# Moving the weight pool of a decoder trunk by 192 bytes, so that its tiles start at the same byte modulo 512 as the transposed input

## The chip, the cores and the metric

The kernel runs on one core of one Trainium2 chip. The metric is device microseconds of the whole program, the median of several runs.

## What is computed

The reference is a decoder trunk of four post-norm layers on 512 tokens of width 1024, in float32. Layers come in the pattern mixer, MLP, mixer, MLP; after each one stands a layer norm of 4^(1/4)·x plus the layer's output.

```python
# mixer 0: stick-breaking attention (8 heads) beside a complex diagonal SSM (32 groups), one output projection
x = layer_norm(ALPHA * x + mixer_sb_ssm(x), ...)
x = layer_norm(ALPHA * x + square(relu(x @ w1[0])) @ w2[0], ...)
# mixer 1: an indexer scores all keys, each query keeps its 128 best, 16 heads attend to those (ALiBi)
x = layer_norm(ALPHA * x + mixer_dsa(x), ...)
x = layer_norm(ALPHA * x + square(relu(x @ w1[1])) @ w2[1], ...)
```

## The kernel before

Every large product is made in three matmuls. A float32 operand is split into a high part in the fp32r type and a low remainder; `mm3` (L129 to L133) then accumulates high·high (L131), high·low (L132 or L133) and low·high. TensorE reads a moving operand of 512 columns, 2048 bytes in each partition, and a stationary operand of 128 columns, 512 bytes in each partition, from SBUF.

Who is moving and who is stationary differs by place:

- Projections to feature-major form (`proj_fm`, the SSM input, the gate): the transposed input `xhi`, `xlo` moves, and the weights `whi`, `wlo` are stationary (L131 to L133). With 512 columns this is the SSM input (`psu`), the queries and keys of both mixers, and groups 1 to 7 of each MLP's first matrix. Group 0 of each MLP and the indexer's projections (`psi`) run in halves of 256 columns.
- Blocks in token-major form: weights move and the activations are stationary. These are the values of mixer 0 (L750 to L752), the output projections (L716 to L718, stationary `xhi`, `xlo`) and the MLP's second matrix (L255 to L257, stationary `hhi`, `hlo`).

Weights pass through three kinds of tile: `raw` (DMA from HBM), `whi` (cast on ScalarE, L104) and `wlo` (remainder, L105). They come from one of two places: the pool "w", which lives through the whole kernel, or a pool that the MLP opens for itself. In the MLP the first matrix's group 0 and nearly all of the second matrix use the MLP's own pool; groups 1 to 7 of the first matrix, and half 0 of the second matrix's last group (48 matmuls in each MLP), use pool "w".

Pools on the left side are stacked in the order in which they are opened: "const", "w", "ln", "x", then each mixer's own. So the size of "const" sets the byte at which everything after it begins, while `xhi`, `xlo`, the MLP's tiles and the SSM's stand on the right side and are not moved by it. Before the change, the start addresses modulo 512, as the built program has them, are:

| tiles | start modulo 512 |
|---|---|
| `xhi`, `xlo` | 480 |
| `raw`, `whi`, `wlo` of pool "w" | 288 |
| the MLP's own `raw`, `whi`, `wlo`, and `hhi`, `hlo` | 480 |
| `ident` | 192 |
| attention tiles `qst`, `kst`, `wt`, `aw` of mixer 0 | 96 to 192 |

Matmul slices start at whole multiples of 512 bytes inside these tiles (the indexer's 64-column key weights apart), so a slice has the residue of its tile.

The order of the work is set by a scheduler that simulates the program as it is built; dependences between tiles, including the reuse of a buffer, shape that order. Around the change it matters in `top_keys` (L981 to L994). For the query blocks it is given, it repeats 16 times: VectorE's MAX (L988) takes the 8 largest scores of a row from `acc` into `top`, and MATCH_REPLACE (L989) overwrites those 8 in `acc`. Block 1 is treated first and alone; blocks 2 and 3 (384 and 512 columns wide) are treated together. `top` has four buffers. When both are done, L993 and L994 make the distance tile `dist` of each block, and `sparse_attention` begins: TensorE makes logits (L1011), VectorE adds `dist` and finds the row minimum (L1018).

Of the kernel before, what the change touches and what calls it, by code (L numbers as in the profile page):

```python
# [8 lines left out]
F32 = mybir.dt.float32  # L9
F32R = mybir.dt.float32r  # L10
AF = mybir.ActivationFunctionType
# [4 lines left out]
P = 128  # L16
# [19 lines left out]
class Trunk:  # L36
    def __init__(self, ctx, tc, a, out):
        self.ctx, self.tc, self.nc, self.a, self.out = ctx, tc, tc.nc, a, out
        self.n = self.n_mlp = self.na = 0
        self.marks = {}  # L40
        self.kept = False
        nc = self.nc
        cp = self.cp = ctx.enter_context(tc.tile_pool(name="const", bufs=1))
        top = ctx.enter_context(tc.tile_pool(name="top", bufs=1, side="right"))
        cp.tile([P, 16], F32, name="pad")
        self.wp = ctx.enter_context(tc.tile_pool(name="w", bufs=1))
        self.psa = ctx.enter_context(tc.tile_pool(name="psa", bufs=1, space=PSUM))
        self.psb = self.psc = None
        self.lnp = ctx.enter_context(tc.tile_pool(name="ln", bufs=1))
        self.xhi = top.tile([P, KT, S], F32R, name="xhi")  # L50
        self.xlo = top.tile([P, KT, S], F32R, name="xlo")
        self.ident = cp.tile([P, P], F32, name="ident")
        self.ident_r = cp.tile([P, P], F32R, name="ident_r")
        self.mhalf = cp.tile([P, 1], F32, name="mhalf")
        self.zero = cp.tile([P, 1], F32, name="zero")
        nc.gpsimd.memset(self.mhalf, -0.5)
        nc.gpsimd.memset(self.zero, 0.0)
        nc.gpsimd.memset(self.ident, 0.0)
        nc.gpsimd.affine_select(out=self.ident, in_=self.ident, pattern=[[-1, P]], compare_op=ALU.not_equal,
                                fill=1.0, base=0, channel_multiplier=1)  # L60
        nc.vector.tensor_copy(self.ident_r, self.ident)
        warm = cp.tile([P, 1], F32, name="warm")
        nc.scalar.activation(warm, self.zero, AF.Exp)

    def open_psb(self):
        self.psc = None
# [914 lines left out]
    def top_keys(self, qbs, ip, accs, drm, dist):  # L981

        vec = self.nc.vector
        for step in range(TOPK // 8):
            for qb in qbs:
                acc = accs[qb]
                top = ip.tile([P, 8], F32, tag="top", bufs=4, name=self.nm("top"))
                vec.max(top, acc)  # L988
                vec.match_replace(acc, top, acc, MARK)  # L989
        for qb in qbs:  # L990
            nk = (qb + 1) * P
            acc = accs[qb]
            vec.tensor_scalar(acc, acc, -3.2e38, BIG, ALU.is_gt, ALU.mult)  # L993
            vec.tensor_tensor(dist[:, qb, :nk], acc, drm[:, S - nk:], ALU.max)  # L994
# [82 lines left out]
```

## Time and profile before

| | |
|---|---|
| median of 3 runs | 1201.22 us (1200.93 to 1202.5) |
| the profiled execution's own time | 1200.24 us |
| its span, first to last instruction | 1198.4 us |
| mean granted TensorE clock | 0.989 |
| TensorE matmul busy | 1157.1 us (97%) |
| VectorE busy | 718.7 us (60%) |
| ScalarE, GpSimd busy | 442.7 us (37%), 192.7 us (16%) |
| chain that ended last, by engine | PE 82%, DVE 11%, DMA 3% |

How to read it: matmuls overlap in the pipe, and the end of one is modelled, so the duration of a matmul row (about 390 ns) is no measure of pace. The distance from the start of one matmul to the start of the next is; it is read from the timeline, whose first column is the start. VectorE rows have real durations. The two MLPs take roughly 250 to 610 us and 835 to 1190 us of the span, mixer 0 the time before, mixer 1 the time between.

### The profile page before, as it was taken

Reading aid. Unit: us, or ns where it says so; the run is one execution under the profiler, and the core shown is the slowest. Engines: PE = TensorE matmul, PEld = TensorE weight load, DVE = VectorE, ACT = ScalarE, POOL = GpSimd, SP = SyncE. Lnnn points to the kernel's source line nnn. Section 1 sums busy time; section 2 is a strip of 40 time slices with the busy share of each in tenths; the row PEclk is TensorE's granted clock in tenths of the full one; section 3 lists DMA queues with packets and bytes.
Section 4 is the critical chain, followed back from the end, with each engine's and each line's share of the span. In section 5 each row is a group of like instructions: output and inputs, shape, how many; then the busy total and the mean of one; then the engine's idle time right before and its main releaser. Section 6 shows DMA issues by size and latency. Waiting matters only on the chain.

```text
span 1198.4 us, 15778 instructions
## 1 busy us (share of the span) xinstructions
PE 1157.1 (97%) x6004; PEld 953.6 (80%) x6004; DVE 718.7 (60%) x1183; ACT 442.7 (37%) x734; POOL 192.7 (16%) x209
## 2 busy tenths in 40 slices
PE   7999998999999999999999989998999999999997
PEld 6878776798888888888898867777988888888886
DVE  7997598675443444444567997559544444444436
ACT  5534486323322332332135457552332332322320
POOL 1044130450000000000021654337000000000001
PEclk9999999999999999999999989999999999999999
DMA  7536772633332332322145850025332332332101
GB/s 239 140 85 142 195 227 54 184 115 106 106 104 72 106 106 71 106 88 54 40 124 142 220 159 1 1 78 175 118 106 71 106 106 73 103 110 83 54 1 71
DMA packets 147307, 127.00 MB, mean 106 GB/s; under 512 B 24352, under 2 KB 115296, under 8 KB 147232
## 3 DMA queue, kind: packets, MB, share of 16 engines
q1 hardware_dynamic: 145552, 123.59, 35.9%
q10 hardware_dynamic: 1680, 2.41, 0.6%
q8 instruction: 47, 0.77, 0.3%
q14 instruction: 28, 0.23, 0.1%
HBM read 105.80 MB, written 5.37 MB: 93 GB/s over the span
## 4 chain that ended last, share of the span: by engine, by line
PE 82%; DVE 11%; DMA 3%; issue 2%; ACT 1%; SPq 1%; POOLq 0%; DVEq 0%; POOL 0%; ACTq 0%
PE psa L133 11%; PE psa L132 11%; PE psa L131 11%; PE psb L257 10%; PE psb L256 10%; PE psb L255 10%; PE pso L824 3%; PE pst L817 2%; PE psl L1011 2%; DVE acc L989 2%; PE psb L716 2%; PE psb L718 2%; PE psb L717 2%; DVE top L988 2%; DVE acc L956 1%
## 5 line engine op out<-in xcount | busy, mean ns | idle before, releaser
L104 ACT CAST whi<-raw 128x1024 fp32r<-128x1024 f32 (+1 forms) x177 | 184.0, 1046 | 490.9 <-PE psb L257 251.2
L105 DVE TENSOR_TENSOR wlo<-raw,whi 128x1024 fp32r<-128x1024 f32 (+1 forms) x142 | 179.7, 1267 | 201.2 <-ACT whi L104 200.8
L132 PE MATMUL psa<-xlo,whi 128*128 128x512 f32 (+1 forms) x720 | 271.6, 378 | 2.4 <-DVE xlo L203 2.4
L133 PE MATMUL psa<-xhi,wlo 128*128 128x512 f32 (+1 forms) x720 | 272.3, 379 | 0.0
L131 PE MATMUL psa<-xhi,whi 128*128 128x512 f32 (+1 forms) x720 | 270.6, 378 | 0.2 <-ACT xhi L202 0.2
L255 PE MATMUL psb<-whi,hhi 128*128 128x512 f32 (+1 forms) x520 | 201.0, 387 | 0.0
L256 PE MATMUL psb<-wlo,hhi 128*128 128x512 f32 (+1 forms) x520 | 200.8, 386 | 0.0
L257 PE MATMUL psb<-whi,hlo 128*128 128x512 f32 (+1 forms) x520 | 193.4, 387 | 0.0
L132 PEld LDWEIGHTS psa<-xlo,whi 128*128 128x128 f32 x720 | 137.1, 190 | 29.4 <-DVE xlo L203 2.6
L262 DVE TENSOR_TENSOR x<-x,psb 128x512 f32<-128x512 f32 (+1 forms) x105 | 69.2, 679 | 150.4 <-PE psb L257 150.2
L133 PEld LDWEIGHTS psa<-xhi,wlo 128*128 128x128 f32 x720 | 137.2, 191 | 27.0
L131 PEld LDWEIGHTS psa<-xhi,whi 128*128 128x128 f32 x720 | 136.6, 191 | 26.8 <-ACT xhi L202 0.5
L105 POOL TENSOR_TENSOR wlo<-raw,whi 128x1024 fp32r<-128x1024 f32 x35 | 93.5, 2684 | 145.8 <-ACT whi L104 136.4
L255 PEld LDWEIGHTS psb<-whi,hhi 128*128 128x128 f32 x520 | 97.7, 188 | 20.1
L256 PEld LDWEIGHTS psb<-wlo,hhi 128*128 128x128 f32 x520 | 97.7, 188 | 20.1
L257 PEld LDWEIGHTS psb<-whi,hlo 128*128 128x128 f32 x520 | 97.6, 188 | 20.1
L184 POOL TENSOR_TENSOR rs<-rs,mhalf 128x1 f32<-128x1 f32 x16 | 21.1, 1317 | 415.4 <-DVE rs L183 415.4
L716 PE MATMUL psb<-whi,xhi 128*128 128x512 f32 x128 | 50.7, 401 | 2.0 <-DVE x L721 2.0
L717 PE MATMUL psb<-wlo,xhi 128*128 128x512 f32 x128 | 50.5, 394 | 0.8 <-DVE wlo L105 0.8
L718 PE MATMUL psb<-whi,xlo 128*128 128x512 f32 x128 | 50.6, 396 | 0.0
L225 DVE TENSOR_TENSOR hlo<-h,hhi 128x512 fp32r<-128x512 f32 x64 | 44.2, 692 | 6.7 <-DVE h L223 0.5
L223 DVE TENSOR_TENSOR h<-r 128x512 f32<-128x512 f32 x64 | 43.8, 684 | 6.9 <-ACT r L222 6.9
(240 smaller groups left out, 1473.6 us busy)
## 6 DMA issues: line engine op xcount, KB each, us to landing
raw<-in_w_dram SPq DMA_DIRECT2D x128, 512.0 KB, 4.1
raw<-in_w_in_dram SPq DMA_DIRECT2D x29, 512.0 KB, 4.4
raw<-in_w_out_dram SPq DMA_DIRECT2D x16, 512.0 KB, 4.7
qst<-hl SPq DMA_DIRECT2D x48, 128.0 KB, 2.9
kst<-hl SPq DMA_DIRECT2D x24, 256.0 KB, 4.6
gb<-in_ln_g_dram SPq DMA_DIRECT2D x4, 512.0 KB, 3.6
gb<-in_ln_b_dram SPq DMA_DIRECT2D x4, 512.0 KB, 5.2
x<-in_x_dram SPq DMA_DIRECT2D x4, 512.0 KB, 6.0
```

The source lines that it names most:

```text
L104: nc.scalar.copy(hi[:, c], raw[:, c])
L105: (eng or nc.vector).tensor_tensor(lo[:, c], raw[:, c], hi[:, c].bitcast(F32), ALU.subtract)
L131: mm(ps, lhi, rhi, start=start, stop=False)
L132: mm(ps, lhi, rlo, start=False, stop=False)
L133: mm(ps, llo, rhi, start=False, stop=stop)
L255: nc.tensor.matmul(ps, lh, whi, start=f + i == 0, stop=False)
L256: nc.tensor.matmul(ps, lh, wlo, start=False, stop=False)
L257: nc.tensor.matmul(ps, ll, whi, start=False, stop=f == 3 and i == len(parts) - 1)
L262: nc.vector.tensor_tensor(xs, xs, ps, ALU.add)
L716: nc.tensor.matmul(ps, chi[:, k, tok], whi, start=i == 0, stop=False)
L717: nc.tensor.matmul(ps, chi[:, k, tok], wlo, start=False, stop=False)
L718: nc.tensor.matmul(ps, clo[:, k, tok], whi, start=False, stop=k == tiles[-1])
```

## The change

The unused tile at the bottom of pool "const" grows by 256 bytes in each partition; two one-column constants become one two-column tile, and the scratch tile for the first activation moves to the layer norm's pool, which gives back 64. Pool "w" and everything stacked on it therefore begins 192 bytes later. `top` has one buffer in place of four.

```diff
-        cp.tile([P, 16], F32, name="pad")
+        cp.tile([P, 80], F32, name="pad")
...
-        self.mhalf = cp.tile([P, 1], F32, name="mhalf")
-        self.zero = cp.tile([P, 1], F32, name="zero")
+        two = cp.tile([P, 2], F32, name="two")
+        self.mhalf, self.zero = two[:, 0:1], two[:, 1:2]
...
-        warm = cp.tile([P, 1], F32, name="warm")
-        nc.scalar.activation(warm, self.zero, AF.Exp)
+        warm = self.lnp.tile([P, 2], F32, tag="mv", bufs=2, name="warm")
+        nc.scalar.activation(warm[:, 0:1], self.zero, AF.Exp)
...
-                top = ip.tile([P, 8], F32, tag="top", bufs=4, name=self.nm("top"))
+                top = ip.tile([P, 8], F32, tag="top", bufs=1, name=self.nm("top"))
```

In the built program of the change, `raw`, `whi` and `wlo` of pool "w" start at 480 modulo 512, `ident` at 448, and the attention tiles of mixer 0 at 288 to 384. `xhi`, `xlo` and the MLP's tiles stay at 480.

The change also moves instructions. The first place is VectorE in `top_keys` for blocks 2 and 3, in the middle of its 16 steps. Here `acc_5236` and `acc_5277` are the scores of block 2 and block 3 before, and `acc_5235` and `acc_5276` the same after. Before:

```order
L988 MAX top_5751<-acc_5236 128x8
L988 MAX top_5754<-acc_5277 128x8
L989 MATCH_REPLACE acc_5236<-top_5751,acc_5236 128x384
L989 MATCH_REPLACE acc_5277<-top_5754,acc_5277 128x512
L988 MAX top_5757<-acc_5236 128x8
L988 MAX top_5760<-acc_5277 128x8
L989 MATCH_REPLACE acc_5236<-top_5757,acc_5236 128x384
L989 MATCH_REPLACE acc_5277<-top_5760,acc_5277 128x512
```

And with the change:

```order
L988 MAX top_5750<-acc_5235 128x8
L989 MATCH_REPLACE acc_5235<-top_5750,acc_5235 128x384
L988 MAX top_5753<-acc_5276 128x8
L989 MATCH_REPLACE acc_5276<-top_5753,acc_5276 128x512
L988 MAX top_5756<-acc_5235 128x8
L989 MATCH_REPLACE acc_5235<-top_5756,acc_5235 128x384
L988 MAX top_5759<-acc_5276 128x8
L989 MATCH_REPLACE acc_5276<-top_5759,acc_5276 128x512
```

Before, the two blocks alternate, so the instruction that an instruction depends on stands two places ahead of it. With the change each MAX and each MATCH_REPLACE depends on the one directly ahead of it, by `acc` or by the single buffer of `top`, and its semaphore wait names that one.

The second place is VectorE at the end of the same search. Before:

```order
L988 MAX top_5823<-acc_5236 128x8
L988 MAX top_5826<-acc_5277 128x8
L989 MATCH_REPLACE acc_5236<-top_5823,acc_5236 128x384
L989 MATCH_REPLACE acc_5277<-top_5826,acc_5277 128x512
L993 TENSOR_SCALAR acc_5236<-acc_5236 128x384
L993 TENSOR_SCALAR acc_5277<-acc_5277 128x512
L994 TENSOR_TENSOR dist<-acc_5236,drm 128x384
```

And with the change:

```order
L988 MAX top_5822<-acc_5235 128x8
L989 MATCH_REPLACE acc_5235<-top_5822,acc_5235 128x384
L988 MAX top_5825<-acc_5276 128x8
L993 TENSOR_SCALAR acc_5235<-acc_5235 128x384
L989 MATCH_REPLACE acc_5276<-top_5825,acc_5276 128x512
L994 TENSOR_TENSOR dist<-acc_5235,drm 128x384
L993 TENSOR_SCALAR acc_5276<-acc_5276 128x512
```

Before, block 3's L994 follows and then the attention's first L1018; with the change the first eight rows of L1018 for block 2 stand ahead of block 3's L994. In the sparse attention that follows, some rows of TensorE, VectorE and ScalarE change places with their neighbours; outside mixer 1 no engine's order differs.

## Rows read from the trace of the kernel before

**Rows 1.** Busy time by stretch: us, PE, PEld, DVE, ACT, POOL, granted clock, DMA share, GB/s

```profile
100.00:137.00 37.00, 37.00 (x225) 32.04 (x225) 22.48 (x42) 15.89 (x25) 6.88 (x6) 0.96 0.53 146
137.00:232.00 95.00, 85.77 (x529) 66.37 (x527) 71.82 (x100) 62.41 (x128) 22.16 (x40) 0.98 0.57 152
232.00:626.00 394.00, 393.57 (x1893) 328.77 (x1894) 203.90 (x262) 114.94 (x152) 31.66 (x35) 1.00 0.32 95
626.00:712.00 86.00, 78.58 (x399) 66.01 (x397) 79.49 (x183) 40.83 (x68) 38.07 (x20) 0.97 0.71 184
833.00:1198.00 365.00, 357.83 (x1668) 297.54 (x1668) 174.25 (x219) 97.37 (x124) 11.08 (x8) 0.99 0.27 85
```

**Rows 2.** Timeline of PE, projection of MLP 0: start, us; first and last of 22

```profile
360.01 0.39 PE L132 MATMUL psa<-xlo,whi 128*128 128x512 f32 x1
...
364.91 0.40 PE L132 MATMUL psa<-xlo,whi 128*128 128x512 f32 x1
```

**Rows 3.** Timeline of PE, second matrix of MLP 0, own pool's weights: first and last of 28

```profile
337.84 0.39 PE L256 MATMUL psb<-wlo,hhi 128*128 128x512 f32 x1
...
343.96 0.39 PE L256 MATMUL psb<-wlo,hhi 128*128 128x512 f32 x1
```

**Rows 4.** Timeline of PE, last group, weights of pool "w": first and last of 11

```profile
593.34 0.39 PE L257 MATMUL psb<-whi,hlo 128*128 128x512 f32 x1
...
595.63 0.40 PE L255 MATMUL psb<-whi,hhi 128*128 128x512 f32 x1
```

**Rows 5.** Timeline of PE, output projection of mixer 1: first and last of 26

```profile
798.86 0.39 PE L717 MATMUL psb<-wlo,xhi 128*128 128x512 f32 x1
...
804.58 0.39 PE L718 MATMUL psb<-whi,xlo 128*128 128x512 f32 x1
```

**Rows 6.** PE groups by line and shape, 232 to 610 us: count, busy us, mean ns

```profile
L131 PE MATMUL psa<-xhi,whi 128*128 128x512 f32 x224 | 88.6, 396 | 0.0
...
L717 PE MATMUL psb<-wlo,xhi 128*128 128x512 f32 x26 | 10.2, 394 | 0.8 <-DVE wlo L105 0.8
```

**Rows 7.** PE groups by line and shape, 0 to 232 us

```profile
L132 PE MATMUL psu<-xlo,whi 128*128 128x512 f32 x32 | 13.0, 425 | 0.0
L752 PE MATMUL psb<-whi,xlo 128*128 128x512 f32 x32 | 12.7, 403 | 0.0
```

**Rows 8.** Timeline of PE, indexer's projection, 256 columns, pool "w": first and last of 37

```profile
614.19 0.28 PE L133 MATMUL psi<-xhi,wlo 128*128 128x256 f32 x1
...
618.27 0.28 PE L133 MATMUL psi<-xhi,wlo 128*128 128x256 f32 x1
```

**Rows 9.** Timeline of PE, group 0 of MLP 0, 256 columns, own pool: first and last of 14

```profile
262.01 0.28 PE L131 MATMUL psa<-xhi,whi 128*128 128x256 f32 x1
...
263.57 0.28 PE L132 MATMUL psa<-xlo,whi 128*128 128x256 f32 x1
```

**Rows 10.** Timeline of PE at the start of the sparse attention, idle time before in brackets

```profile
712.58 5.11 PE L1011 MATMUL psl<-kst,qst 128*128 128x384 f32 x20 [5.27 <-DVE pst L1018]
```

**Rows 11.** Timeline of DVE, search in block 1 alone

```profile
636.76 0.43 DVE L988 MAX8 top<-acc 128x8 f32<-128x256 f32 x1
637.23 0.09 DVE L989 MATCH_VALUE_LOAD acc<-top,acc 128x8 f32 x1
637.31 0.41 DVE L989 MATCH_REPLACE8 acc<-top,acc 128x256 f32<-128x256 f32 x1
637.75 0.43 DVE L988 MAX8 top<-acc 128x8 f32<-128x256 f32 x1
```

**Rows 12.** Timeline of DVE, search in blocks 2 and 3, one of 16 steps

```profile
678.35 1.14 DVE L988 MAX8 top<-acc 128x8 f32<-128x384 f32 x2
679.40 0.07 DVE L989 MATCH_VALUE_LOAD acc<-top,acc 128x8 f32 x1
679.46 0.54 DVE L989 MATCH_REPLACE8 acc<-top,acc 128x384 f32<-128x384 f32 x1
679.92 0.08 DVE L989 MATCH_VALUE_LOAD acc<-top,acc 128x8 f32 x1
...
680.58 1.14 DVE L988 MAX8 top<-acc 128x8 f32<-128x384 f32 x2
```

**Rows 13.** DVE groups by line and shape, 676 to 712 us

```profile
L994 DVE TENSOR_TENSOR dist<-acc,drm 128x512 f32<-128x512 f32 x1 | 0.7, 680 | 0.0
```

## The prediction

> **What bounds the kernel now.** I read the busy time by stretch first [rows 1]. The two MLP stretches have TensorE busy for 393.57 of 394 us and 357.83 of 365 us, so there whatever a matmul takes goes straight into the time. From 626 to 712 us it is the other way round: TensorE is busy 78.58 of 86 us and VectorE 79.49. The end of that stretch says who is late: TensorE stands idle for 5.27 us, released by VectorE's L1018 [rows 10], and L1018 can only begin when the search of `top_keys` has filled `dist`. From 137 to 232 us TensorE has 9 us of holes [rows 1].
>
> Then I read the pace of matmuls, from start to start in the timeline, because their durations overlap. All have 512 columns and the full clock; they differ in the residue (start modulo 512) of the moving and of the stationary tile:
>
> - moving 480, stationary 288 (projection): 4.90 us for 21 steps, 233.3 ns each [rows 2]
> - both 480 (second matrix, MLP's own pool): 6.12 us for 27 steps, 226.7 ns [rows 3]
> - moving 288, stationary 480 (the same three lines, weights from pool "w"): 2.29 us for 10 steps, 229 ns [rows 4]
> - moving 288, stationary 480 (output projection): 5.72 us for 25 steps, 228.8 ns [rows 5]
>
> The third against the second is nearly the experiment that the change makes: same lines, same shapes, same stationary tiles, and only the pool of the weights differs. The third and the fourth are different lines and stages with equal residues and equal pace. So I take the pace to follow the two residues, and 226.7 ns as the pace when both are 480.
>
> With 256 columns it runs the other way: 480 and 288 give 4.08 us for 36 steps, 113.3 ns [rows 8]; both 480 give 1.56 us for 13 steps, 120.0 ns [rows 9]. Alignment is not good as such; it is good at 512 columns.
>
> **The change, part by part.**
>
> *Projections with 512 columns* go from 233.3 to 226.7 ns, 6.6 ns less. An MLP has 224 of each of three lines [rows 6], the second MLP the same by its code: 1344 matmuls, 8.9 us, all of it on the path, since TensorE has no holes there. The supply keeps up: in the first MLP's stretch ScalarE works 115 of 394 us and the DMA share is 0.32 [rows 1]. In mixer 0 the SSM input is 3 × 32 matmuls [rows 7], 0.6 us. Of the 192 of queries and keys the half that lies in 100 to 137 us, where TensorE has no hole, counts: 0.7 us. The gate's 48 lie in 137 to 232 us, among VectorE's and ScalarE's waits, and I count nothing. The 240 of mixer 1 (queries and keys, about 1.6 us) lie in 626 to 712 us, and there VectorE is last: TensorE only waits longer. Also nothing.
>
> *Blocks whose weights move from pool "w"* gain 2.1 to 2.3 ns. Values of mixer 0, 3 × 32 [rows 7]: 0.2 us. Half 0 of the last group, 96 matmuls in both MLPs: 0.2 us. Output projections: 3 × 26 in the stretch after 232 us [rows 6] and the 192 of mixer 1: 270 × 2.1 ns, 0.6 us; the rest lie among holes.
>
> *The indexer's projection with 256 columns* loses 6.7 ns for each of 96 matmuls just ahead of the search: 0.6 us slower. Its 48 matmuls with 64-column weights get residues that no row shows; I bound them by the same 6.7 ns either way, 0.3 us, and take 0.
>
> *Transposes, logits and weighted values* get new residues as well, which no run of rows shows in the pair they will have. I take 0; the bound is the largest shift between the rows above, 6.6 ns, for the 128 logit matmuls, under 1 us either way.
>
> Together: 8.9 + 0.6 + 0.7 + 0.2 + 0.2 + 0.6 − 0.6 = 10.6 us gained.
>
> *One buffer of `top`.* Before, an instruction of the pair search depends on the one two places ahead. The pair of MAX takes 1.14 us but the next instruction starts 1.05 us after it; the first MATCH_REPLACE ends at 680.00 and the next load of values starts at 679.92 [rows 12]. Neighbours overlap by 0.08 to 0.09 us. In block 1, searched alone, each instruction waits for the one directly ahead, as all will with the change, and there MAX ends at 637.19 and its successor starts at 637.23; MATCH_REPLACE ends at 637.72 and the next MAX starts at 637.75 [rows 11]: a gap of 0.03 to 0.04 us. Overlap turned into gap is 0.12 us at each of four boundaries, so a step of 2.23 us [rows 12] becomes 2.71; 16 steps cost 7.7 us. The end of the search gives some back: block 3's L994, 0.68 us [rows 13], no longer stands ahead of the first L1018; I take 0.6. That leaves 7.1 us, and all of it is on the path, because TensorE already waits there. The first logits are queued before the hole, so nothing else of TensorE can fill it: the reordered rows all come after.
>
> After the hole, which grows from 5 to about 14 us (7.1, and the 1.6 us by which TensorE is early), the 20 logit matmuls took 5.11 us [rows 10], 256 ns each for 384 columns: more than the 233.3 ns that 512 columns take in rows 2, so they run partly at the lower of the two clock levels already. A longer hole can change how long that lasts by a microsecond or so either way; I take 0.
>
> *The constants and the scratch tile* cost nothing: the same instructions on the same engines, at the start, while TensorE waits for its first weights. The order differs nowhere outside mixer 1. The neighbours that change places in the sparse attention run while TensorE is the bound; I take 0, with 1 us either way.
>
> **Sum:** −10.6 + 7.1 = −3.5 us. Against the profiled execution's own 1200.24 us that is 1196.7. The median of the runs stands 1.0 us above that execution, so the forecast for a median is 1197.7 us. Its own range, from 5.5 to 6.7 ns for the projections and the "either way" terms, is 1194.5 to 1200.5.
>
> **Rivals.**
>
> *The residue does nothing, and the search is longer.* The pace could belong to something else that differs between the rows: how far apart the tiles lie, or the line. Then nothing is gained and the 7.1 us of waits remain: 1208.3 us, slower. It decides below a gain of 4.4 ns a projection matmul (7.1 of 10.6, times 6.6). Against it stand rows 3 and 4, the same lines at two paces, and rows 4 and 5, two lines at one. For it: the MLP's pool lies elsewhere in SBUF too, and no row has a 512-column projection at 480 and 480. Chance 0.12. The Trainium skill would have it so: its page "TensorE: Matmul & The Clock Gate", section "Back-to-back issue gap", gives N ÷ 2.4 + 2.5 ns, 215.8 ns for 512 columns, with no place for an address, and "SBUF — State Buffer", section "SBUF: two separate sides", says that TensorE never waits on another reader. By that rule alignment would bring nothing; the trace disagrees, with three paces, all above it.
>
> *Part of the gain.* Projections improve by half, as if the role of a tile mattered beside its residue: 5.3 us gained, 7.1 lost, 1203.0 us. Chance 0.14.
>
> *The waits of the search cost nothing.* If the semaphore's gap vanished in the overlap, only the gain remains, with the 0.6 us at the end: 1190.0 us. Against it stands block 1's search, which shows the gap in this kernel [rows 11]. Chance 0.08. The Trainium skill's page "VectorE: DVE Perf Modes", section "The DRAIN you can't avoid", states that a semaphore after each of eight copies cost nothing extra; by that rule this rival would hold. Rows 11 and 12 differ by 0.12 us a boundary, so here the trace speaks against it.
>
> **How the numbers follow.** The forecast has 0.66. A measurement of this kernel can tell about 0.2%, 2.4 us, from no change: faster means below 1198.8, slower above 1203.6. Of the forecast's 0.66, 0.50 lies below 1198.8, 0.15 within and 0.01 above; the third rival adds 0.08 to faster; the half gain splits into 0.10 within and 0.04 above; the first rival adds 0.12 to slower. That gives 0.58, 0.25 and 0.17. The range takes in the half gain with a microsecond to spare, and leaves out the first rival and most of the third: 1191.0 to 1204.0.
>
> **What would show it.** In the profile after: projections of the MLPs at 226.7 ns from start to start, and the lines of the second matrix at one pace throughout; the indexer's 256-column matmuls at 120 ns; a step of the pair search at 2.7 us with a gap between its rows; the hole before the sparse attention at 12 to 15 us; the first MLP's TensorE stretch about 4.8 us shorter. I am wrong if projections stay at 233 ns, if they reach another pace, if the search keeps 2.23 us a step, or if the longer hole is filled.

## The result, and the profile after

The changed kernel takes 1195.43 us in the median (1194.85 to 1195.7) against 1201.08 for the kernel before on the same chip: a ratio of 0.9943, 95% interval 0.9923 to 0.9963. It is faster, inside the range and 2.3 us below the forecast. One execution of this kernel (1618.94 us, at a granted clock of 0.653) and one of run 1 below (3974.93 us) were far slower; they count in the two medians, which are 1195.17 and 1186.31 us without them, and in no range or ratio. The profiled execution of the changed kernel took 1195.17 us, 5.07 less than that of before.

Three places carry it. First the pace of a projection, from the timeline of TensorE of the changed kernel in MLP 0: first and last of 24 matmuls in a row.

```profile
351.74 0.39 PE L131 MATMUL psa<-xhi,whi 128*128 128x512 f32 x1
...
356.96 0.39 PE L133 MATMUL psa<-xhi,wlo 128*128 128x512 f32 x1
```

5.22 us for 23 steps are 227.0 ns, where [rows 2] gave 233.3; the second matrix kept its pace of [rows 3]. The indexer's 256-column matmuls went the other way, as forecast. First and last of 23 in the same timeline:

```profile
608.78 0.28 PE L131 MATMUL psi<-xhi,whi 128*128 128x256 f32 x1
...
611.42 0.28 PE L132 MATMUL psi<-xlo,whi 128*128 128x256 f32 x1
```

2.64 us for 22 steps, 120.0 ns, against 113.3 in [rows 8].

Second the search. One step for blocks 2 and 3 in VectorE's timeline, which answers to [rows 12]:

```profile
671.51 0.56 DVE L988 MAX8 top<-acc 128x8 f32<-128x384 f32 x1
672.11 0.09 DVE L989 MATCH_VALUE_LOAD acc<-top,acc 128x8 f32 x1
672.18 0.54 DVE L989 MATCH_REPLACE8 acc<-top,acc 128x384 f32<-128x384 f32 x1
672.76 0.69 DVE L988 MAX8 top<-acc 128x8 f32<-128x512 f32 x1
673.49 0.09 DVE L989 MATCH_VALUE_LOAD acc<-top,acc 128x8 f32 x1
673.57 0.67 DVE L989 MATCH_REPLACE8 acc<-top,acc 128x512 f32<-128x512 f32 x1
674.28 0.56 DVE L988 MAX8 top<-acc 128x8 f32<-128x384 f32 x1
```

The two MAX no longer stand side by side, each MAX and each load of values begins 0.04 us after the row ahead has ended, and a step takes 2.77 us instead of 2.23.

Third what follows from that, in TensorE's timeline, which answers to [rows 10]:

```profile
698.28 1.56 PE L1011 MATMUL psl<-kst,qst 128*128 128x384 f32 x8
714.47 4.01 PE L1011 MATMUL psl<-kst,qst 128*128 128x384 f32 x16 [14.62 <-DVE pst L1018]
```

Eight logit matmuls stand ahead of the hole and the ninth ends it, as before; the hole has grown from 5.27 to 14.62 us.

The ledger, with places as TensorE reaches them in the two profiled executions. The forecast's terms are sorted into the same stretches; the 78 output projections after mixer 0 are counted in the first:

| stretch | before, us | after, us | measured | forecast |
|---|---|---|---|---|
| start to the first L255 of MLP 0 | 276.95 | 276.92 | −0.03 | −1.66 |
| first to last L255 of MLP 0 | 332.59 | 327.56 | −5.03 | −4.55 |
| to the first L953 (indexer's scores) | 20.18 | 20.57 | +0.39 | +0.6 |
| to the ninth logit matmul L1011 | 82.86 | 89.42 | +6.56 | +7.1 |
| to the last L716 (sparse attention, output) | 114.40 | 112.53 | −1.87 | −0.4 |
| to the first L255 of MLP 1 | 31.82 | 31.87 | +0.05 | 0 |
| first to last L255 of MLP 1 | 331.51 | 326.38 | −5.13 | −4.55 |
| the rest, outside the span included | 9.93 | 9.92 | −0.01 | 0 |
| sum | 1200.24 | 1195.17 | −5.07 | −3.5 |

### The profile page after: what moved, and what is told of

Same layout as the page of the kernel before. It is cut to its first block, busy times and chain, and to the rows that moved or that the text cites. A ratio compares the mean times of both kernels' runs of the same rounds, so it can differ in the third digit from the quotient of the medians.

```text
span 1193.4 us, 15777 instructions
## 1 busy us (share of the span) xinstructions
PE 1141.6 (96%) x6004; PEld 952.2 (80%) x6004; DVE 724.5 (61%) x1183; ACT 443.2 (37%) x734; POOL 193.2 (16%) x209
## 4 chain that ended last, share of the span: by engine, by line
PE 82%; DVE 11%; DMA 3%; issue 2%; ACT 1%; SPq 1%; POOLq 0%; DVEq 0%; POOL 0%; ACTq 0%
PE psa L132 11%; PE psa L133 11%; PE psa L131 11%; PE psb L257 10%; PE psb L256 10%; PE psb L255 10%; PE pso L824 3%; PE pst L817 2%; DVE acc L989 2%; DVE top L988 2%; PE psl L1011 2%; PE psb L716 2%; PE psb L718 2%; PE psb L717 2%; DVE sh L498 1%
## 5 line engine op out<-in xcount | busy, mean ns | idle before, releaser
L105 DVE TENSOR_TENSOR wlo<-raw,whi 128x1024 fp32r<-128x1024 f32 (+1 forms) x142 | 179.8, 1268 | 194.3 <-ACT whi L104 194.0
L132 PE MATMUL psa<-xlo,whi 128*128 128x512 f32 (+1 forms) x720 | 267.1, 372 | 2.4 <-DVE xlo L203 2.4
L133 PE MATMUL psa<-xhi,wlo 128*128 128x512 f32 (+1 forms) x720 | 267.6, 372 | 0.0
L131 PE MATMUL psa<-xhi,whi 128*128 128x512 f32 (+1 forms) x720 | 265.9, 372 | 0.2 <-ACT xhi L202 0.2
L255 PE MATMUL psb<-whi,hhi 128*128 128x512 f32 (+1 forms) x520 | 200.6, 386 | 0.0
L257 PE MATMUL psb<-whi,hlo 128*128 128x512 f32 (+1 forms) x520 | 193.0, 386 | 0.0
L132 PEld LDWEIGHTS psa<-xlo,whi 128*128 128x128 f32 x720 | 136.4, 189 | 25.7 <-DVE xlo L203 2.6
L133 PEld LDWEIGHTS psa<-xhi,wlo 128*128 128x128 f32 x720 | 136.3, 189 | 23.0
L131 PEld LDWEIGHTS psa<-xhi,whi 128*128 128x128 f32 x720 | 135.7, 190 | 23.2 <-ACT xhi L202 0.5
L105 POOL TENSOR_TENSOR wlo<-raw,whi 128x1024 fp32r<-128x1024 f32 x35 | 93.6, 2686 | 144.8 <-ACT whi L104 143.7
L257 PEld LDWEIGHTS psb<-whi,hlo 128*128 128x128 f32 x520 | 97.7, 188 | 19.6
L255 PEld LDWEIGHTS psb<-whi,hhi 128*128 128x128 f32 x520 | 97.7, 188 | 19.5
L184 POOL TENSOR_TENSOR rs<-rs,two 128x1 f32<-128x1 f32 x16 | 21.1, 1318 | 408.8 <-DVE rs L183 408.7
L716 PE MATMUL psb<-whi,xhi 128*128 128x512 f32 x128 | 50.6, 400 | 2.3 <-DVE x L721 2.3
```

The lines of the kernel that those rows point to most:

```text
L105: (eng or nc.vector).tensor_tensor(lo[:, c], raw[:, c], hi[:, c].bitcast(F32), ALU.subtract)
L131: mm(ps, lhi, rhi, start=start, stop=False)
L132: mm(ps, lhi, rlo, start=False, stop=False)
L133: mm(ps, llo, rhi, start=False, stop=stop)
L255: nc.tensor.matmul(ps, lh, whi, start=f + i == 0, stop=False)
L257: nc.tensor.matmul(ps, ll, whi, start=False, stop=f == 3 and i == len(parts) - 1)
```

## The experiments

The theory: the pace follows the residues of the two tiles, and the waits of the single `top` are a price of their own, added to it. Runs 1 to 3 and 5 take the two apart; 4 and 6 to 11 move the pool to seven other residues, to see what about a residue counts; 12 takes what was learned and leaves the rest of the kernel as it was.

In all but 2 and 12, `top` has four buffers which stand in the layer norm's pool, under two tags of that pool:

```diff
-                top = ip.tile([P, 8], F32, tag="top", bufs=1, name=self.nm("top"))
+                top = self.lnp.tile([P, 8], F32, tag=("st", "mv")[(step * len(qbs) + qbs.index(qb)) % 2], bufs=2, name=self.nm("top"))
```

**1 and 5: the residues alone.** The changed kernel with only that line different.

> The weight pool at 480 as in the change, but the search keeps four buffers for its eight maxima (slots of the layer norm's pool, idle at that time). If alignment and search add up, the projections stay at 226.7 ns and the pair search is back at 2.23 us a step: the hole before the sparse attention shrinks from 14.6 to 6 to 7 us and the time is 1195.4 - 6.5 = 1189 us (1187.5 to 1191). Rival: the longer hole of the change cost nothing, because the sparse attention made it good (its stretch was 1.9 us shorter in the change) and the rest is lost elsewhere: then 1193 to 1195.5 us.

Measured: 1187.25 us, ratio 0.9888 (0.9869 to 0.9907). The kernel ran again as e5, for a profile.

> The same kernel as e1_align_only (weight pool at residue 480, four buffers of top), for a profile. Theory (the residues and the search's waits are two prices that add up): about 1187 us as there; projections and output projections at 226.7 ns; the step of the pair search back at 2.23 us and the stretch from the indexer's transposed input (L953) to the ninth logit matmul some 5.5 to 6.5 us shorter than the 89.4 us of the changed kernel, so 83 to 84. Rival (the waits of the search are not what the second part costs, but the new order of the rows): step 2.23 and yet a stretch of over 87 us.

Measured: 1187.0 us, ratio 0.9889 (0.9872 to 0.9905). From the timelines of VectorE and of TensorE in e5:

```profile
681.23 1.14 DVE L988 MAX8 top<-acc 128x8 f32<-128x512 f32 x2
682.29 0.07 DVE L989 MATCH_VALUE_LOAD acc<-top,acc 128x8 f32 x1
682.35 0.67 DVE L989 MATCH_REPLACE8 acc<-top,acc 128x512 f32<-128x512 f32 x1
682.95 0.08 DVE L989 MATCH_VALUE_LOAD acc<-top,acc 128x8 f32 x1
683.01 0.54 DVE L989 MATCH_REPLACE8 acc<-top,acc 128x384 f32<-128x384 f32 x1
683.47 0.68 DVE L988 MAX8 top<-acc 128x8 f32<-128x512 f32 x1
```

```profile
702.12 5.76 PE L1011 MATMUL psl<-kst,qst 128*128 128x384 f32 x20 [4.10 <-DVE pst L1018]
```

The MAX stand in pairs again, a step is 2.24 us, and the hole is 4.10. The stretch from the first L953 to the ninth logit matmul takes 78.46 us: not the 83 to 84 expected but 5 less. The theory stands, yet its account of this stretch was incomplete; the table under run 2 takes it apart.

**2: the single buffer alone.**

```diff
-                top = ip.tile([P, 8], F32, tag="top", bufs=4, name=self.nm("top"))
+                top = ip.tile([P, 8], F32, tag="top", bufs=1, name=self.nm("top"))
```

> The kernel before with one buffer of top, nothing moved by 192 bytes. If the waits of the search are a price of their own, a step of the pair search takes 2.77 us as in the change and the time is 1201.1 + 4.7 to 6.5 = 1206 to 1208 us, with the projections still at 233.3 ns. Rival: the waits are hidden in this kernel, because TensorE is later there without the alignment: 1201 to 1203 us.

Measured: 1206.25 us, ratio 1.005 (1.0033 to 1.0067): 5.7 us slower, the projections still at 233 ns. TensorE's timeline:

```profile
719.25 1.97 PE L1011 MATMUL psl<-kst,qst 128*128 128x384 f32 x5 [11.20 <-DVE pst L1018]
```

The stretch in three pieces, in us, by the starts of rows:

| kernel | first to last L953 | to the last MAX (L988) | to the ninth logit matmul |
|---|---|---|---|
| before | 33.80 | 44.42 | 4.64 |
| e2, one buffer alone | 33.62 | 52.06 | 2.94 |
| after | 32.18 | 54.29 | 2.95 |
| e5, residues alone | 31.74 | 43.76 | 2.96 |

The middle column prices the waits: e2 over before is 7.64, where the forecast had 7.7. The changed kernel pays 2.23 more, and one row shows why. VectorE's and GpSimd's timelines of the changed kernel:

```profile
666.84 2.59 DVE L994 TENSOR_TENSOR dist<-acc,drm 128x256 f32<-128x256 f32 x1
```

```profile
666.75 2.40 POOL L105 TENSOR_TENSOR wlo<-raw,whi 128x1024 fp32r<-128x1024 f32 x1 [0.85 <-ACT whi L104]
```

Block 1's L994 takes 0.41 us in e2. Here it starts 0.09 us after a GpSimd instruction of 2.40 and ends 0.28 after it: it waited for it. The Trainium skill, "SBUF — State Buffer", section "SBUF: two separate sides", has the rule: a VectorE operation with two inputs in SBUF and a GpSimd operation reading SBUF take an exclusive lock, and whoever comes second stands still until the first has ended. This row agrees.

**3: equal residues, but not 480.** Pool "w" back at 288, and `xhi`, `xlo` and the MLP's tiles moved to 288.

```diff
-        cp.tile([P, 80], F32, name="pad")
+        cp.tile([P, 32], F32, name="pad")
...
-        self.xlo = top.tile([P, KT, S], F32R, name="xlo")
+        self.xlo = top.tile([P, KT, S], F32R, name="xlo"); top.tile([P, 48], F32, name="pad2")
```

> The weight pool back at 288; instead xhi, xlo, the MLP's tiles and all others on the right side move down by 192 bytes, to 288 as well; the search has four buffers as in e1. If the pace follows the difference of the two residues, all 512-column products run at 226.7 ns, the 256-column ones at 120, and the time equals e1's within 1.5 us: 1189. Rival: the byte 480 itself is what helps (its place against the 512-byte line), then the pairs at 288 and 288 run at some other pace, 229 to 233 ns, and the second matrix, at 226.7 before, gets slower: 1198 to 1206 us.

Measured: 1185.54 us, ratio 0.9873 (0.9856 to 0.9889), against 1187.0 for e5. The run of projections from 351.65 to 356.86 us has 226.5 ns a step: no residue is good by itself; the pair counts.

**4 and 6 to 8: other distances.** Only the pad differs: 64 columns put the pool at 416 (e4), 48 at 352 (e6). The pools at 448 (e7) and 0 (e8) come the same way.

```diff
-        cp.tile([P, 80], F32, name="pad")
+        cp.tile([P, 64], F32, name="pad")
```

> As e1, but the weight pool starts at 416 modulo 512, 64 bytes short of xhi. If equality of the residues is what counts, the projections fall back to 229 to 233 ns and the time lies 4 to 9 us over e1's, 1193 to 1198. If only a coarse block of 128 bytes counts (416 and 480 lie in different ones), the same; if the place inside 128 bytes counts, not: 288 and 480 differ by 64 there too. Rival: any residue close to xhi's is as good, then 226.7 ns and e1's time.

Measured: 1192.9 us in one run, at the lower edge of what I expected. From TensorE's timeline, first and last of 23 projections, and of 15 matmuls of the output projection, where the weights move and `xhi`, `xlo` are stationary:

```profile
351.77 0.39 PE L131 MATMUL psa<-xhi,whi 128*128 128x512 f32 x1
...
356.80 0.39 PE L132 MATMUL psa<-xlo,whi 128*128 128x512 f32 x1
...
796.71 0.40 PE L718 MATMUL psb<-whi,xlo 128*128 128x512 f32 x1
...
799.97 0.40 PE L717 MATMUL psb<-wlo,xhi 128*128 128x512 f32 x1
```

228.6 ns with the moving tile 64 above the stationary one, 232.9 with it 64 below. Before, it was the other way about: 233.3 with the moving tile 192 above [rows 2], 228.8 with it 192 below [rows 5]. The sign matters.

> Weight pool at residue 352, 128 below the moving tiles' 480; four buffers of top. Theory S (pace follows the signed difference of the starts, moving less stationary, with 0 the fastest and 192 at 233.3 ns, 64 at 228.5): projections (480/352) at 230 to 231.5 ns, MLP about 5 us longer than aligned, 1191 to 1194 us in all. Rival Z (only equal residues are special, all others alike): projections at 228.5 or 233.3 ns, as one of the two seen. Rival W (the weights' residue alone sets it): L716 and L255, whose stationary tile stays at 480, would run at 226.7 ns.

> Weight pool at residue 448, 32 below the moving tiles' 480; four buffers of top. Theory S (graded by the signed difference): projections 227 to 228 ns, time within 2 us of the aligned kernel's 1187. Rival Z (only equality is special): projections at 228.5 ns or more, 1190 to 1192 us. For the opposite sign, L716 with moving 448 and stationary 480, S gives something between 226.7 and the 234 ns measured at minus 64.

> Weight pool at residue 0, 32 above the moving tiles' 480 if the residues wrap, 480 below if they don't; four buffers of top. Theory S with wrap: projections as the opposite sign of a small difference, 229 to 234 ns; L716 (moving 0, stationary 480) about 227.5 ns, the mirror of the pool at 448. Without wrap both would be far from equal and over 229 ns. Rival B (a start on a multiple of 512 is good as such): both at 226.7 ns. Time 1188 to 1196 us.

Measured, in one run each: 1198.02, 1199.96 and 1199.23 us, with projections at 232.2, 233.5 and 233.5 ns: all three times lie above those expected. Theory S, a price graded by the distance, falls: e7 at a distance of 32 is as slow as before at 192. Nor is equality the only good value, as rival Z has it, since 64 lies between. Rivals W and B fall too: the output projections of e6 and e8 take 232 and 234 ns. The values fit if distances are counted modulo 256: then plus 64 and minus 192 are the same distance, and minus 64 and plus 192.

**9 to 11: the rule modulo 256, put at risk.** Pads of 16 columns and of none (224 and 160), and of 56 (384).

> Weight pool at residue 224, so 256 away from the moving tiles' 480 in both directions; four buffers of top. The seven differences seen so far (moving less stationary: 0 at 226.7 ns; 64 and minus 192 at 228 to 230; 32, 128, 192, minus 32, minus 64, minus 128 at 232 to 234) fit a rule of the difference modulo 256, where 0 is fastest, 64 next and the rest alike. Theory M (modulo 256): 226.7 ns for projections (480/224) and for L716 (224/480), the 256-column form at 120, 1186 to 1189 us in all, as with the pool at 480. Rival E (only equality modulo 512 is special): 232 to 234 ns, 1196 to 1200 us.

> Weight pool at residue 160, 320 below the moving tiles' 480; four buffers of top. Theory M (modulo 256): 320 counts as 64, so projections 228 to 230 ns; L716 (160/480) counts as 192 and runs at 232 to 234; 1190 to 1193 us. Rival E (equality modulo 512 alone, the two middle values by chance): projections 232 to 234 ns, 1196 to 1200 us.

> Weight pool at residue 384, 96 below the moving tiles' 480; four buffers of top. Theory M with 0 and 64 as the only good differences: projections (96) and L716 (minus 96, that is 160) both at 232 to 234 ns, 1196 to 1200 us. Rival G (a graded curve round 64): projections between 228.5 and 232.6 ns, 1191 to 1196 us.

Measured: e9 1186.13 us, ratio 0.9874 (0.9858 to 0.9891). From its TensorE timeline, first and last of 24 projections and of 15 matmuls of the output projection:

```profile
351.67 0.39 PE L131 MATMUL psa<-xhi,whi 128*128 128x512 f32 x1
...
356.88 0.39 PE L133 MATMUL psa<-xhi,wlo 128*128 128x512 f32 x1
...
789.67 0.39 PE L718 MATMUL psb<-whi,xlo 128*128 128x512 f32 x1
...
792.85 0.39 PE L717 MATMUL psb<-wlo,xhi 128*128 128x512 f32 x1
```

226.5 and 227.1 ns, with tiles 256 apart. e10: 1192.81 us in one run, within its 1190 to 1193. e11: 1202.23 us in one run, its pace as theory M has it, its time 2 us above what I expected. All ten pools, by moving start less stationary start modulo 256; the projections from the timeline between 352 and 357 us (of before, [rows 2]), the output projections as the median step of the kernel's whole trace:

| difference | projections, ns | output projections, ns |
|---|---|---|
| 0 | 227.0 (after), 226.5 (e3), 226.5 (e9) | 227 (after, e3, e9) |
| 32 | 233.5 (e7) | 234 (e8) |
| 64 | 228.6 (e4), 228.7 (e10) | 229 (before) |
| 96 | 233.0 (e11) | none |
| 128 | 232.2 (e6) | 232 (e6) |
| 160 | none | 234 (e11) |
| 192 | 233.3 (before) | 234 (e4), 234.5 (e10) |
| 224 | 233.5 (e8) | 235 (e7) |

Where both columns have a value they agree within 1.5 ns, though weights are stationary in one and moving in the other.

**12: only what is needed.** At 224 the pool fits under the pad of before, because merging the constants and moving the scratch tile already gives back 64 bytes. So `top` keeps its four buffers in its own pool; of the change nothing remains but this:

```diff
-        self.mhalf = cp.tile([P, 1], F32, name="mhalf")
-        self.zero = cp.tile([P, 1], F32, name="zero")
+        two = cp.tile([P, 2], F32, name="two")
+        self.mhalf, self.zero = two[:, 0:1], two[:, 1:2]
...
-        warm = cp.tile([P, 1], F32, name="warm")
-        nc.scalar.activation(warm, self.zero, AF.Exp)
+        warm = self.lnp.tile([P, 2], F32, tag="mv", bufs=2, name="warm")
+        nc.scalar.activation(warm[:, 0:1], self.zero, AF.Exp)
```

> Weight pool at residue 224 with the pad of before and `top` in its own pool with four buffers: only the constants share a tile and the scratch tile moves. Theory (modulo 256, and nothing of the gain needs the padding or the one buffer): 512-column projections at 227 ns, step of the pair search 2.23 us, and the same search as before; 1186 to 1189 us, the upper half if the 1.5 us that the runs with `top` in the layer norm's pool gain at the end of the search are due to their order. Rival (the place of `top` counts in itself): a step other than 2.23 us, or a time over 1190 us.

Measured: 1187.27 us (1186.44 to 1190.01), ratio 0.9883 (0.9865 to 0.99). The median step of the projections is 227 ns, that of the search 2.24 us. TensorE's hole is that of before:

```profile
704.47 5.49 PE L1011 MATMUL psl<-kst,qst 128*128 128x384 f32 x20 [5.66 <-DVE pst L1018]
```

It beats the kernel before by 14 us and the changed kernel by 7 to 8 (by the two ratios and by the two medians; they did not run side by side), with pool "w" 64 bytes below where it was instead of 192 above. Runs 3, 5 and 9 are as fast; the intervals overlap.

## Why the prediction was right, step by step

**The pace follows the two residues: right.** In the two MLPs the L131, L132 and L133 of the ledger's stretches sum to 313.57 us before and 304.63 after: 8.94 us, where the forecast had 8.9. What it took for the reason, equal residues modulo 512, was too narrow; runs 9 and 10 show modulo 256. The rival in which the residue does nothing is out by run 5, and the half gain by the paces. The formula that the prediction quotes for that rival (the Trainium skill, "TensorE: Matmul & The Clock Gate", section "Back-to-back issue gap") is given there for a single isolated matmul, so it was no rule for a stream like this one.

**Half 0 of the last group: mis-sized.** It was to give 0.2 us in both MLPs. The second matrix gained 0.57 and 0.66 us, 1.2 in all: L255 to L257 of the ledger's stretches sum to 343.56 us before and 342.33 after. Steps of [rows 4]'s kind had a mean of 230 ns over the kernel, not 229, and the other steps of these lines went from a mean of 227.4 to 226.7. The latter moved mostly at one place: ahead of the last groups, the first six second-matrix matmuls behind each run of projections have a mean step of 231.3 ns before and 227.0 after, and from the seventh on it is 226.6 and 226.7. What holds those six up no run shows: in e8, with projections as slow, their mean is 228.0.

**The projections of mixer 1 "also nothing": nearly right, with too simple a reason.** I had VectorE last in the whole stretch from 626 to 712 us. It is last only at its end: the search cannot finish before the indexer's scores are there, and their matmuls (L953) are queued among projections. From first to last L953 the changed kernel took 1.62 us less (e5: 2.06). But only 60 of the 240 projections stand between them, and most of the gain is the clock. Before, the granted clock was at the lower of its two levels (0.50, 1.2 GHz) from 645.4 to 648.8 us, and soon after that VectorE waited for a score, which it does not in the changed kernel:

```profile
652.03 0.62 DVE L956 SCALAR_TENSOR_TENSOR acc<-rel,wi,acc 128x384 f32<-128x384 f32 x1 [1.19 <-ACT rel L955]
```

Busy time with the columns of [rows 1]: of before in those 3.4 us, then of the changed kernel and of e8 around the stretch from the first to the last L953:

```profile
645.40:648.80 3.40, 3.40 (x12) 2.72 (x11) 2.85 (x6) 2.40 (x6) 0.00 (x0) 0.50 0.41 122
```

```profile
625.00:658.00 33.00, 30.78 (x185) 27.55 (x186) 28.03 (x60) 18.29 (x39) 7.13 (x4) 1.00 0.63 160
```

```profile
631.00:662.00 31.00, 29.75 (x182) 26.45 (x181) 27.39 (x58) 17.59 (x37) 6.64 (x4) 1.00 0.62 161
```

e8 has projections as slow as before but no such fall of the clock, and took 31.18 us, less than the changed kernel's 32.18. The steps of the 60 projections sum to 15.37 us before, 13.98 in e8 and 13.78 in the changed kernel: about 1.4 us is the clock's, 0.2 the residues'. The fall is in none of the five profiled kernels at difference 0 and in six of the eight others, so whether alignment helps to avoid it stays open.

**Waits of the search, +7.7: right in size** (7.64 in e2), by two errors. The step grew by 0.54 us instead of 0.48, which makes 8.6 for 16 steps: I had missed that the two MAX of a pair also overlapped, by 0.11 us (0.56 and 0.69 alone, 1.14 together). And the search before had a collision of its own, which e2 has not: block 1's L993 took 1.44 us while GpSimd ran an L105, in e2 it takes 0.29. The Trainium skill's finding that a semaphore after each of eight copies cost nothing extra ("VectorE: DVE Perf Modes", section "The DRAIN you can't avoid") does not carry over to this step: run 2 changes nothing in the search but the order of its rows and what each waits for, and pays 0.54 us a step.

**"The end of the search gives some back", 0.6: too small.** It gave 1.69 us (4.64 to 2.95). VectorE's timeline after:

```profile
711.52 0.69 DVE L988 MAX8 top<-acc 128x8 f32<-128x512 f32 x1
712.13 0.34 DVE L993 TENSOR_SCALAR acc<-acc 128x384 f32<-128x384 f32 x1
712.39 0.08 DVE L989 MATCH_VALUE_LOAD acc<-top,acc 128x8 f32 x1
712.46 0.68 DVE L989 MATCH_REPLACE8 acc<-top,acc 128x512 f32<-128x512 f32 x1
713.05 0.55 DVE L994 TENSOR_TENSOR dist<-acc,drm 128x384 f32<-128x384 f32 x1
713.51 0.42 DVE L993 TENSOR_SCALAR acc<-acc 128x512 f32<-128x512 f32 x1
713.85 0.55 DVE L1018 CUSTOM_DVE_ANT_0 pw<-psl,dist 128x384 f32<-128x384 f32 x1
```

I counted block 3's L994, which is gone from here. But block 2 is also done a turn earlier: its L993 runs in the gap of block 3, where before both L993 (1.27 us as a pair) and both L994 (1.15) stood behind the last MATCH_REPLACE. The order showed that ahead of time; I had priced one row of it. And 0.6 of the 1.69 us is not the order's. Before, block 2's L993 stood beside a GpSimd row:

```profile
709.71 1.27 DVE L993 TENSOR_SCALAR acc<-acc 128x384 f32<-128x384 f32 x2
```

```profile
709.16 1.27 POOL L739 TENSOR_TENSOR hl<-ev,hl 128x512 fp32r<-128x512 f32 x1
```

In run 12, with the same order, GpSimd's row had ended 0.26 us before the pair began; the pair takes 0.69 us and the whole piece 4.06:

```profile
702.19 0.69 DVE L993 TENSOR_SCALAR acc<-acc 128x384 f32<-128x384 f32 x2
```

**A collision at 0: missed.** L994 behind L105 cost 2.2 us. So the stretch's +6.56 is −1.62 + 9.87 − 1.69, three misses that nearly cancel against 7.1. That is luck: a fall of the clock is in the first, and what GpSimd happened to run beside a row in the other two.

**Mixer 0, −1.5: not seen in this pair of profiles, and not settled.** Both lost time at one place where the clock fell. Busy time from 190 to 212 us of the changed kernel and of e5 (PE, PEld, DVE, ACT, POOL; then the granted clock):

```profile
190.00:212.00 22.00, 18.48 (x135) 14.35 (x135) 17.81 (x29) 15.72 (x36) 0.89 (x9) 0.92 0.00 1
```

```profile
190.00:212.00 22.00, 18.49 (x150) 14.26 (x148) 19.24 (x30) 15.98 (x36) 0.89 (x9) 1.00 0.01 2
```

For the same busy time, 135 matmuls at a mean of 0.92 and 150 at 1.00. The dip comes in some profiles and not in others, whatever the residues. With a dip between 194 and 231 us, the way from mixer 0's first attention matmul (L789) to MLP 0 takes 130.9 to 131.9 us (eight profiles: before, after, 3, 4, 6, 8, 10, 11); without one 129.2 to 129.8 (five: 2, 5, 7, 9, 12). Of those five the three with difference 0 reach MLP 0 at 275.5, 275.6 and 276.5 us, the two others at 277.4 and 277.6. That is the size forecast, from five profiles; within the dipped ones the spread is as large as the effect, and before, without any gain, reaches L789 as early as e5 (146.05 us both).

**Sparse attention 0: it gave 1.5 us more than its output projections.** About 0.5 us is the new order's: TensorE's first wait for ScalarE's L818, ahead of L824, is 0.57 us before and in runs 3 to 12. In the changed kernel and in run 2 it is under 0.1. Before, and after:

```profile
719.39 0.66 PE L824 MATMUL pso<-pt,v 128*64 128x128 f32 x8 [0.57 <-ACT pt L818]
```

```profile
720.18 0.66 PE L824 MATMUL pso<-pt,v 128*64 128x128 f32 x8
```

Run 2, with the old residues, saves 0.5 us over the stretch (113.89 for 114.40). Part of the rest is the clock: it rose again 4.5 us after the restart before, 3.1 after (run 2: 5.4). I did not take the two apart further.

The sign came out right because the one large doubtful term was well supported: the same lines at two paces, with another pool the only difference [rows 3, 4]. The size came out near by luck, because the errors, +1.6 us at the start and −3.2 elsewhere, have both signs.

## What to carry to other kernels

A matmul's pace can depend on where its two operands start in SBUF; compare start-to-start distances of equal shapes from different pools before believing that a TensorE-bound stretch is at its floor, and move a pool by a few bytes to see. Ask what a shift costs in buffers before choosing it: here minus 64 bytes would have served as well as plus 192 and left `top` its four, 7 to 8 us better. An engine that is last at the end of a stretch need not be last at its start. And before crediting a microsecond between two profiles to a change, compare the granted clock of the stretch: in the indexer's scores it was 1.4 of 1.6 us.

## What was not expected of the hardware

For 512-column matmuls on fp32r tiles only the signed difference of the two starts modulo 256 told the runs apart: 0 took 226.5 to 227 ns, 64 took 229, and every other multiple of 32 between 232 and 235. With 256 columns, 0 is a loss: 120 ns, as at 96, against 115.5 at 64 and 114 at 192 (means over the indexer's projections with 128 stationary columns, in the changed kernel, e11, e4 and before). What in the reading of operands makes it so, no run here shows.
